# Three split passes for one full-precision product in the second half of a bidirectional recurrence

## The chip, the cores and the metric

The kernel runs on one core of a Trainium2 chip. The metric is the time of one execution on the device in microseconds (us), the median of several runs. Engines are named as in the profile: PE is TensorE's matmul (PEld its load of the stationary operand), DVE is VectorE, ACT is ScalarE, POOL is GpSimd, and SP is SyncE, on whose queue nearly all transfers (DMAs) of this kernel are issued, in program order.

## The reference

One layer over 2048 tokens of width 1024, all in float32: a modulated layer norm, one input projection, two mixers side by side (a bidirectional gated recurrence of 8 heads of 128, and a 2-D neighbourhood attention of 16 heads of 64), one output projection, and a second layer norm. What matters here is one direction of the recurrence for one head:

```python
def step(state, xs):
    qc, kc, vc, dc = xs
    o = jnp.einsum('bhtd,bhdv->bhtv', qc, state)
    state = dc[..., None] * state + jnp.einsum('bhtd,bhtv->bhdv', kc, vc)
    return state, o
...
o = direction(zf_fw, lb_fw, False) + direction(zf_bw, lb_bw, True)
o = _rmsnorm(o.transpose(0, 2, 1, 3), norm_g).reshape(B, S, HG_WIDTH)
return o.astype(g_in.dtype) * jax.nn.silu(g_in)
```

The backward direction runs over the flipped tokens, so the outputs of the first 1024 tokens need a state that comes from the last 1024.

## The kernel before

**Stages.** The program goes through a start (modulation, layer norm, first projections), the attention on the first tokens, the recurrence, the attention on the rest, and the output projection. The recurrence goes over 16 steps: `half` 0 (tokens 0 to 1023) for heads `u` = 0 to 7, then `half` 1 (tokens 1024 to 2047) for the same heads. Each step has two groups `g` of 512 tokens.

**Who sets the order.** `weave` interleaves two generators: `hgrn(u, half, ...)`, the recurrence of one head, and `hgrn_dense`, the projection of the next head (or, in the last step, `border_dense` for the attention that follows). PE's order is what the two generators emit, instruction by instruction, and nothing moves it afterwards (`manual_schedule` for PE). The orders on DVE, ACT, POOL and SP are made by a scheduler when the program is built, which goes by its own estimate of times; so a few more instructions in one place can swap neighbours there.

**Weights.** Each projection matmul in float32 is done in three passes of `fp32r` operands (L278): weights and activations are split into a high part (an ACT copy to `fp32r`) and a low part (a DVE subtraction), and high x high, high x low and low x high are added up in PSUM. Weights come through four raw buffers `wr`, issued on SP at L262, split at L268 (ACT) and L269 (DVE).

**The tail of a head.** After the body of `hgrn`, what is left of a head is handed on as a generator `tail` (`hgrn_tail`), of which the next head's `hgrn` takes a piece at each `next(tail, None)`. Half 0's tail stores, for each group, the output so far (`op_d`, L658), the gate (`sg_d`, L659), and the queries already multiplied by the decay up to the half's end (`qb_d`, L664). Half 1's tail first finishes its own two groups with `rms_out`, and then, with the backward state `R` that its tokens leave behind, goes over the first half's two groups: it loads `qb` (L671), `op` (L672) and the gate (L673), multiplies `R` by `qb` on PE (L676) with both operands as plain float32, adds `op` on DVE (L677) and calls `rms_out`. That one squares on ACT (L345), splits the squares on DVE (L347, L349), sums them over partitions with two `fp32r` matmuls (L354, L355), takes the root on ACT (L357, L358), multiplies on DVE by the output (L359) and by the gate (L361), and stores (L362).

**Buffers.** The three loads are tiles of 128 x 512 under the tag `cl`, for which there are 3 buffers, given out in turn. So group 1's `qb` takes the buffer of group 0's `qb` (free after L676), its `op` takes that of group 0's `op` (free after L359, its last reader), and its gate that of group 0's gate (free after L361). The states `R` are tiles `Sb` with 5 buffers.

Of the kernel before, what the change touches and what calls it, by code (L numbers as in the profile page):

```python
# [10 lines left out]
F32 = mybir.dt.float32  # L11
F32R = mybir.dt.float32r
U32 = mybir.dt.uint32
AF = mybir.ActivationFunctionType
ALU = mybir.AluOpType
# [4 lines left out]
P = 128  # L20
KT = D // P
HALF = 1024
GRP = 512
NHEAD = 8
# [14 lines left out]
def body(ctx: ExitStack, tc: tile.TileContext, t):  # L39
    nc = tc.nc  # L40
    dve, act, pool, pe = nc.vector, nc.scalar, nc.gpsimd, nc.tensor
    dma = nc.sync.dma_start
# [22 lines left out]
    def dram(name, shape, dt=F32):  # L65
        if name in t:
            return t[name]
        return nc.dram_tensor(name, shape, dt, kind="Internal").ap()
# [4 lines left out]
    c_d = dram("c_d", (D,))  # L73
    hs = [dram(f"hs{k}", (P, 2, HALF)) for k in range(KT)]
    op_d = [dram(f"op{i}", (P, HALF)) for i in range(NHEAD)]
    qb_d = [dram(f"qb{i}", (P, HALF)) for i in range(NHEAD)]
    sg_d = [dram(f"sgd{i}", (P, HALF)) for i in range(NHEAD)]
    nq_d = [dram(f"nq{i}", (P, 512)) for i in range(NPAIR)]
    nk_d = [dram(f"nk{i}", (P, 768)) for i in range(NPAIR)]
# [8 lines left out]
    def nm(s):  # L88
        cnt[0] += 1
        return f"{s}_{cnt[0]}"  # L90

    def tl(tag, dt=F32, shape=None):
        if tag in cur["smap"]:
            tag = cur["smap"][tag]
            return sh.tile([P, 512], dt, tag=tag, name=nm(tag), bufs=SH[tag])
        return cur["pool"].tile([P, 512] if shape is None else shape, dt, tag=tag, name=nm(tag), bufs=cur["bufs"].get(tag, 1))
# [4 lines left out]
    def ps(tag="mx"):  # L101
        if tag == "pj":
            return pp.tile([P, 512], F32, tag=tag, name=nm("pj"))
        tag = cur["map"].get(tag, tag)
        return cur["psum"].tile([P, 512], F32, tag=tag, name=nm("ps"), bufs=cur["ps"][tag])
# [237 lines left out]
    def rms_out(u, g, o_sb, sg, tok, rest=False):  # L343
        sq = tl("t")
        act.activation(sq, o_sb, AF.Square)  # L345
        sh_ = tl("rh", F32R)
        dve.tensor_copy(sh_, sq)  # L347
        sl_ = tl("rl", F32R)
        dve.tensor_tensor(sl_, sq, sh_, op=ALU.subtract)  # L349
        yield  # L350
        if rest:
            yield
        pss = ps("ss")
        pe.matmul(pss, ones, sh_, start=True, stop=False)  # L354
        pe.matmul(pss, ones, sl_, start=False, stop=True)  # L355
        r = tl("t")
        act.activation(r, pss, AF.Ln, scale=1.0 / 128.0, bias=eps_rms)  # L357
        act.activation(r, r, AF.Exp, scale=-0.5)  # L358
        dve.tensor_mul(r, r, o_sb)  # L359
        yv = tl("t")  # L360
        dve.tensor_tensor(yv, r, sg, op=ALU.mult)  # L361
        dma(yT[u][:, tok:tok + 512], yv)  # L362
# [60 lines left out]
    def hgrn(u, half, st, tail):  # L423
# [197 lines left out]
        for _ in tail:  # L621
            pass
        return hgrn_tail(u, half, sgs, ubs, decs, qibs, os_, decb_all)

    HSUM = 54

    def hgrn_tail(u, half, sgs, ubs, decs, qibs, os_, decb_all):

        R = None
        if half == 0:  # L630
            ds_ = tl("dsuf", shape=[P, 8])
            pool.memset(ds_[:, 7:8], 1.0)
            for b in range(6, -1, -1):
                dve.tensor_mul(ds_[:, b:b + 1], ds_[:, b + 1:b + 2], decb_all[:, b + 1:b + 2])
        obs = {}
        for g in (1, 0):
            po = os_[g]
            pend = []
            for b in range(3, -1, -1):
                sl = slice(b * P, (b + 1) * P)  # L640
                if R is not None:
                    pend.append((sl, R))
                if half == 0 and g == 0 and b == 0:
                    break
                rn = tl("Sb", shape=[P, P])
                if R is None:
                    dve.tensor_copy(rn, ubs[g][:, sl])
                else:
                    dve.scalar_tensor_tensor(rn, R, decs[1, g][:, b:b + 1], ubs[g][:, sl], op0=ALU.mult, op1=ALU.add)
                R = rn  # L650
            yield
            for sl, r in pend:
                pe.matmul(po[:, sl], r, qibs[1, g][:, sl], start=False, stop=True, skip_group_check=True)
            ob = tl("t")
            act.activation(ob, po, AF.Copy)
            tk = slice(g * 512, (g + 1) * 512)
            if half == 0:
                dma(op_d[u][:, tk], ob)  # L658
                dma(sg_d[u][:, tk], sgs[g])  # L659
                qb = tl("t")  # L660
                for b in range(4):
                    sl = slice(b * P, (b + 1) * P)
                    dve.tensor_scalar(qb[:, sl], qibs[1, g][:, sl], ds_[:, g * 4 + b:g * 4 + b + 1], 1.0, op0=ALU.mult, op1=ALU.mult)
                dma(qb_d[u][:, tk], qb)  # L664
            else:
                yield from rms_out(u, g, ob, sgs[g], HALF + g * 512, g == 0)
        if half == 1:
            for g in range(2):
                tk = slice(g * 512, (g + 1) * 512)
                qb, o1, sg = tl("cl"), tl("cl"), tl("cl")  # L670
                dma(qb, qb_d[u][:, tk])  # L671
                dma(o1, op_d[u][:, tk])  # L672
                dma(sg, sg_d[u][:, tk])  # L673
                yield
                po = ps("pc")
                pe.matmul(po, R, qb, start=True, stop=True)  # L676
                dve.tensor_tensor(o1, po, o1, op=ALU.add)  # L677
                yield from rms_out(u, g, o1, sg, g * 512)

# [777 lines left out]
    with psum_phase("h", *HPS), phase("h", HB, SMH), tc.manual_schedule(engines={mybir.EngineType.PE}):  # L1457
        hgrn_init()
        tail = iter(())
        for i in range(16):  # L1460
            half, u = divmod(i, 8)
# [246 lines left out]
```

## Time and profile before

| | |
|---|---|
| median of 3 runs | 2613.16 us (2608.88 to 2614.05) |
| the profiled execution, its own time | 2611.2 us |
| its span, first to last instruction | 2609.4 us |
| granted TensorE clock, mean | 0.995 |
| PE busy | 2565.7 us (98%) |
| DVE busy | 1741.0 us (67%) |
| ACT busy | 1432.1 us (55%) |
| DMA, mean over the span | 114 GB/s |
| L676, the product with the carried state | 16 products, 32 matmul instructions, 1206.4 to 1717.3 us |

All views are of that one profiled execution, and times in them are counted from its span's start. A busy time of PE is of pipelined matmuls, so PE that is 98% busy may still hold room; the chain of waits shows how long each piece of PE's work really keeps the next one back.

### The profile page before, as it was taken

The page shows a single profiled execution, that of the slowest core. Times are in us where ns is not written, and L with a number is a line of the kernel's source. Part 1 is how long each engine was busy: PE and PEld are TensorE (multiplying, and loading weights), DVE is VectorE, ACT ScalarE, POOL GpSimd, SP SyncE. Part 2 cuts the span into 40 slices and gives each one's busy share as a digit, 9 for nine tenths or more (in the row PEclk, how much of TensorE's full clock was granted, in tenths as well). Part 3 has the DMA queues.
Part 4 walks back from the last instruction along what each step waited for, and adds up shares of the span by engine and source line. Part 5 has one row for each costly group of instructions (what it writes and reads, how often), then busy time and mean ns, then how long its engine had stood idle before and what let it go on. Part 6 is the DMA issues. An engine that isn't in the chain of part 4 may idle for free.

```text
span 2609.4 us, 45888 instructions
## 1 busy us (share of the span) xinstructions
PE 2565.7 (98%) x17180; PEld 2153.9 (83%) x17180; DVE 1741.0 (67%) x4362; ACT 1432.1 (55%) x2853; POOL 108.3 (4%) x143
## 2 busy tenths in 40 slices
PE   8999999999999999999999999999999999999998
PEld 6888788878888888888888888888888887788887
DVE  7445445377777778877778777555777778558443
ACT  5533445376666666666667666455777777431110
POOL 0000000000000000000000000000000000032221
PEclk9999999999999999999999999999999999999999
DMA  7566454212111126212211222354455556444331
GB/s 291 143 207 154 137 177 139 90 50 74 58 65 66 58 78 226 77 49 74 80 62 58 74 73 82 108 147 134 123 143 142 142 138 167 124 152 130 97 97 57
DMA packets 225919, 296.40 MB, mean 114 GB/s; under 512 B 28839, under 2 KB 117543, under 8 KB 224551
## 3 DMA queue, kind: packets, MB, share of 16 engines
q1 hardware_dynamic: 225695, 293.46, 36.8%
q8 instruction: 135, 2.21, 0.4%
q14 instruction: 89, 0.73, 0.1%
HBM read 218.18 MB, written 66.99 MB: 109 GB/s over the span
## 4 chain that ended last, share of the span: by engine, by line
PE 93%; DVE 3%; DMA 2%; ACT 2%; issue 0%; SPq 0%; DVEq 0%; ACTq 0%
PE pj L278 52%; PE pj L291 6%; PE ps L1534 4%; PE ps L1535 4%; PE ps L1533 4%; PE ps L1112 3%; PE ps L1090 3%; PE ps L482 2%; PE ps L474 2%; PE ps L1041 2%; PE ps L549 1%; PE ps L278 1%; PE ps L573 1%; PE ps L1048 1%; PE ps L521 1%; PE ps L575 1%
## 5 line engine op out<-in xcount | busy, mean ns | idle before, releaser
L278 PE MATMUL pj<-h,wh 128*128 128x512 f32 x3984 | 1270.8, 400 | 3.6 <-ACT wh L825 1.9
L278 PEld LDWEIGHTS pj<-h,wh 128*128 128x128 f32 x3984 | 723.4, 189 | 155.4 <-issue 13.8
L278 PE MATMUL pj<-h,wl 128*128 128x512 f32 x1992 | 781.9, 393 | 0.0
L278 PEld LDWEIGHTS pj<-h,wl 128*128 128x128 f32 x1992 | 374.7, 188 | 83.1 <-DVE wl L801 0.4
L1062 ACT ACTIVATE pbuf<-pbuf,mx 128x480 f32<-128x480 f32 (+5 forms) x256 | 152.4, 596 | 109.9 <-DVE mx L1057 109.0
L1057 DVE CUSTOM_DVE_ANT_1 pbuf<-ps,bias 128x480 f32<-128x480 f32 (+5 forms) x256 | 129.1, 540 | 103.1 <-PE ps L1048 46.1
L291 PE MATMUL pj<-wh,h 128*128 128x256 f32 x1024 | 195.7, 286 | 0.3 <-ACT e L774 0.3
L291 PEld LDWEIGHTS pj<-wh,h 128*128 128x128 f32 x1024 | 163.0, 191 | 4.0 <-issue 1.3
L269 DVE TENSOR_TENSOR wl<-wr,wh 128x512 fp32r<-128x512 f32 x192 | 131.6, 686 | 48.0 <-ACT wh L268 47.6
L268 ACT ACTIVATE wh<-wr 128x512 fp32r<-128x512 f32 x192 | 120.0, 626 | 74.2 <-PE pj L278 66.5
L291 PE MATMUL pj<-wl,h 128*128 128x256 f32 x512 | 144.8, 283 | 0.0
L1096 ACT ACTIVATE pt<-ps 120x384 f32<-120x384 f32 (+3 forms) x128 | 65.2, 509 | 121.6 <-PE ps L1090 121.3
L1090 PE MATMUL ps<-ident,pbuf 128*128 128x128 f32 (+2 forms) x832 | 114.4, 275 | 4.5 <-DVE pbuf L1067 3.7
L1094 DVE COPY pt<-ps 120x384 f32<-120x384 f32 (+3 forms) x128 | 74.9, 585 | 63.0 <-PE ps L1090 62.0
L1090 PEld LDWEIGHTS ps<-ident,pbuf 128*128 128x128 f32 (+2 forms) x832 | 97.6, 137 | 22.6 <-issue 2.5
L468 DVE TENSOR_TENSOR de<-e,de 128x512 f32<-128x512 f32 x64 | 44.3, 692 | 95.1 <-ACT de L467 95.1
L1509 ACT ACTIVATE yh<-yr 128x512 fp32r<-128x512 f32 x52 | 32.7, 629 | 133.0 <-PE ps L1534 115.8
L1067 DVE TENSOR_SCALAR pbuf<-pbuf,mx 128x480 f32<-128x480 f32 (+5 forms) x256 | 101.1, 413 | 3.8
L1582 DVE TENSOR_TENSOR vt<-ps,gt 128x512 f32<-128x512 f32 x24 | 16.5, 692 | 130.7 <-PE ps L1535 130.7
L774 ACT ACTIVATE e<-pj 128x512 f32<-128x512 f32 x97 | 57.8, 596 | 79.8 <-PE pj L278 73.1
L291 PEld LDWEIGHTS pj<-wl,h 128*128 128x128 f32 x512 | 97.9, 191 | 1.4 <-issue 0.5
L449 DVE TENSOR_TENSOR_SCAN c<-c,g 128x128 f32<-128x128 f32 x256 | 88.6, 407 | 10.7 <-ACT c L439 10.7
(283 smaller groups left out, 4707.5 us busy)
## 6 DMA issues: line engine op xcount, KB each, us to landing
wr<-in_w_in SPq DMA_DIRECT2D x276, 256.0 KB
yr<-yq SPq DMA_DIRECT2D x64, 256.0 KB
bias<-tint SPq DMA_DIRECT2D x24, 480.0 KB
x<-in_x SPq DMA_DIRECT2D x32, 256.0 KB
ada<-in_ada_m SPq DMA_DIRECT2D x8, 1024.0 KB
wr<-in_w_v SPq DMA_DIRECT2D x32, 256.0 KB
nv<-vt SPq DMA_DIRECT2D x32, 256.0 KB
hs<-s SPq DMA_DIRECT2D x32, 256.0 KB
```

What stands on the lines that cost most here:

```text
L268: act.activation(hi, raw, AF.Copy)
L269: dve.tensor_tensor(lo, raw, hi, op=ALU.subtract)
L278: pe.matmul(pz, a, b, start=(k == 0 and n == 0), stop=(k == KT - 1 and n == 2))
L291: pe.matmul(pzs[tp][:, i * 256:(i + 1) * 256], a, b, start=(k == 0 and n == 0 and i == 0), stop=(k == KT - 1 and n == 2), skip_group_check ...
L449: dve.tensor_tensor_scan(c[:, sl], c[:, sl], L[:, sl], 0.0, op0=ALU.add, op1=ALU.subtract)
L1057: return dve.tensor_tensor_reduce(s[:, 0:nk].rearrange("p (r c) -> p r c", c=kw), sc[:, 0:nk].rearrange("p (r c) -> p r c", c=kw), bt[:, 0 ...
L1062: act.activation(s[:, 0:nk], s[:, 0:nk], AF.Exp, scale=-1.0, bias=mx[:, 0:1], accum_out=mx[:, 1:2])
L1067: dve.tensor_scalar(s[:, 0:nk], s[:, 0:nk], mx[:, 2:3], 1.0, op0=ALU.mult, op1=ALU.mult)
L1090: pe.transpose(ptp[0:cw, c * P:(c + 1) * P], s[:, c * cw:(c + 1) * cw], ident)
L1533: pe.matmul(pz, yh[:, kk], wh, start=first, stop=False)
L1534: pe.matmul(pz, yh[:, kk], wl, start=False, stop=False)
L1535: pe.matmul(pz, yl[:, kk], wh, start=False, stop=last)
```

## The change

In half 0 the decayed queries `qb` are split before they are stored: ACT copies them to `fp32r` (`qh`), DVE subtracts (`ql`), and both are stored, so that `qb_d` has twice the size. In half 1 the state `R` is split on DVE into `Rh` and `Rl`, both queries' parts are loaded, and the one float32 product becomes three `fp32r` products. All of `qh`, `ql`, `op` and the gate are `cl` tiles, four in place of three for 3 buffers; the gate's tile is taken, and its load issued, after the products.

```diff
-    qb_d = [dram(f"qb{i}", (P, HALF)) for i in range(NHEAD)]
+    qb_d = [dram(f"qb{i}", (P, 2, HALF)) for i in range(NHEAD)]
...
-                qb = tl("t")
+                qb, qh, ql = tl("t"), tl("cl", F32R), tl("cl", F32R)
                 for b in range(4):
                     sl = slice(b * P, (b + 1) * P)
                     dve.tensor_scalar(qb[:, sl], qibs[1, g][:, sl], ds_[:, g * 4 + b:g * 4 + b + 1], 1.0, op0=ALU.mult, op1=ALU.mult)
-                dma(qb_d[u][:, tk], qb)
+                act.activation(qh, qb, AF.Copy)
+                dve.tensor_tensor(ql, qb, qh, op=ALU.subtract)
+                dma(qb_d[u][:, 0, tk], qh.bitcast(F32))
+                dma(qb_d[u][:, 1, tk], ql.bitcast(F32))
             else:
                 yield from rms_out(u, g, ob, sgs[g], HALF + g * 512, g == 0)
         if half == 1:
+            Rh, Rl = tl("Sb", F32R, [P, P]), tl("Sb", F32R, [P, P])
+            dve.tensor_copy(Rh, R)
+            dve.tensor_tensor(Rl, R, Rh, op=ALU.subtract)
             for g in range(2):
                 tk = slice(g * 512, (g + 1) * 512)
-                qb, o1, sg = tl("cl"), tl("cl"), tl("cl")
-                dma(qb, qb_d[u][:, tk])
+                qh, ql, o1 = tl("cl", F32R), tl("cl", F32R), tl("cl")
+                dma(qh.bitcast(F32), qb_d[u][:, 0, tk])
+                dma(ql.bitcast(F32), qb_d[u][:, 1, tk])
                 dma(o1, op_d[u][:, tk])
-                dma(sg, sg_d[u][:, tk])
                 yield
                 po = ps("pc")
-                pe.matmul(po, R, qb, start=True, stop=True)
+                for i, (a, b) in enumerate(((Rh, qh), (Rh, ql), (Rl, qh))):
+                    pe.matmul(po, a, b, start=i == 0, stop=i == 2)
+                sg = tl("cl")
+                dma(sg, sg_d[u][:, tk])
                 dve.tensor_tensor(o1, po, o1, op=ALU.add)
                 yield from rms_out(u, g, o1, sg, g * 512)
```

In the changed file the stores stand at L666 and L667, the split of `R` at L672 and L673, the loads of `qh`, `ql`, `op` and the gate at L677, L678, L679 and L685, the products at L683 and the addition at L686; later lines stand 9 lower.

**On SP**, the loads for the two groups of one head in half 1 (head 1). Before, from the store that ends the head's own last group: `cl_2568`, `cl_2569` and `cl_2570` are group 1's `qb`, `op` and gate, and `cl_2717` is the next head's first `qb`.

```order
L362 DMA yq0<-t_2546_13604 128x512 [waits DVE_49]
L671 DMA cl_2568_13736<-qb1 128x512 [waits PE_49]
L262 DMA wr_2679_14251<-in_w_in 128x512 [waits DMAHW3_49,DVE_49]
L262 DMA wr_2682_14257<-in_w_in 128x512 [waits DMAHW4_49,DVE_49]
L672 DMA cl_2569_13737<-op1 128x512 [waits DVE_49]
L362 DMA yq0<-t_2567_13733 128x512 [waits DMAHW5_49,DVE_49]
L673 DMA cl_2570_13738<-sgd1 128x512 [waits DMAHW6_49]
L671 DMA cl_2717_14437<-qb2 128x512 [waits DMAHW7_49,DMAHW1_49,PE_49]
```

Now, the same piece: `cl_2596` is group 0's gate, `cl_2607`, `cl_2608`, `cl_2609` and `cl_2625` are group 1's `qh`, `ql`, `op` and gate.

```order
L362 DMA yq0<-t_2582_13696 128x512 [waits DVE_49]
L685 DMA cl_2596_13782<-sgd1 128x512 [waits PE_49]
L677 DMA cl_2607_13836<-qb1 128x512 [waits PE_49]
L262 DMA wr_2719_14355<-in_w_in 128x512 [waits DMAHW5_49,DVE_49]
L262 DMA wr_2722_14361<-in_w_in 128x512 [waits DMAHW6_49,DVE_49]
L678 DMA cl_2608_13837<-qb1 128x512 [waits DMAHW7_49,DVE_49]
L362 DMA yq0<-t_2606_13833 128x512 [waits DMAHW0_49,DVE_49]
L679 DMA cl_2609_13838<-op1 128x512 [waits DMAHW3_49,DMAHW1_49]
L685 DMA cl_2625_13904<-sgd1 128x512 [waits DMAHW7_49,DMAHW2_49,PE_49]
```

The place in the queue where `op` stood (after the two weight loads, waiting for DVE) now has `ql`; `op` has gone behind the store, to where the gate stood, and group 0's gate is now loaded only after its product.

**On PE**, group 1's product of the same head, before:

```order
L278 MATMUL pj_2584_13778<-h_1886_10379,wl_2583_13775 128x512
L676 MATMUL ps_2585_13800<-cl_2568_13736,Sb_2499_13385 128x512 [waits DMAHW1_49,Activation_49]
L474 MATMUL ps_2589_13809<-ident_71,de_2577_13760 128x128 [waits PE_49]
L474 MATMUL ps_2589_13809<-ident_71,de_2577_13760 128x128 x3
L278 MATMUL pj_2584_13778<-h_1888_10383,wh_2582_13774 128x512
```

and now:

```order
L278 MATMUL pj_2623_13878<-h_1910_10439,wl_2622_13875 128x512
L683 MATMUL ps_2624_13900<-cl_2607_13836,Sb_2583_13699 128x512 [waits DMAHW4_49,Activation_49]
L683 MATMUL ps_2624_13900<-cl_2608_13837,Sb_2583_13699 128x512 [waits DMAHW7_49]
L683 MATMUL ps_2624_13900<-cl_2607_13836,Sb_2584_13700 128x512
L474 MATMUL ps_2629_13913<-ident_71,de_2616_13860 128x128 [waits PE_49]
L474 MATMUL ps_2629_13913<-ident_71,de_2616_13860 128x128 x3
L278 MATMUL pj_2623_13878<-h_1912_10443,wh_2621_13874 128x512
```

The product stands at the same place among the projection matmuls, but its second pass waits for a transfer of its own, that of `ql` (`cl_2608`).

**On ACT**, the square L345 of group 1, in the same head, before:

```order
L476 ACTIVATE ke_2590_13814<-ps_2589_13809 128x512 [waits PE_49]
L467 ACTIVATE de_2661_14171<-c_2641_14094 128x128 x4
L345 ACTIVATE t_2586_13803<-cl_2569_13737 128x512 [waits DVE_49]
L389 ACTIVATE vt_2597_13841<-pj_2584_13778 128x512 [waits PE_49]
L268 ACTIVATE wh_2644_14105<-wr_2643_14103 128x512 [waits DMAHW6_49,PE_49]
```

and now:

```order
L476 ACTIVATE ke_2630_13918<-ps_2629_13913 128x512 [waits PE_49]
L467 ACTIVATE de_2701_14275<-c_2681_14198 128x128 x4
L389 ACTIVATE vt_2637_13945<-pj_2623_13878 128x512 [waits PE_49]
L345 ACTIVATE t_2626_13907<-cl_2609_13838 128x512 [waits DVE_49]
L268 ACTIVATE wh_2684_14209<-wr_2683_14207 128x512 [waits DMAHW0_49,PE_49]
```

L389, the copy of a finished projection out of PSUM, has moved ahead of the square; this stands so in heads 0 to 5, and not in the last two.

## The prediction

> **What bounds the kernel now.** I read the page first, for the span and the chain that ended last.
>
> ```profile
> span 2609.4 us, 45888 instructions
> PE 93%; DVE 3%; DMA 2%; ACT 2%; issue 0%; SPq 0%; DVEq 0%; ACTq 0%
> ```
>
> The chain lies on PE for 93% of the span. The execution took 2611.2 us, 1.8 us more than its span, and is 2.0 us quicker than the median of the runs, 2613.16 us. I sum against the execution and carry the difference over to the median. Next, the engines' busy time by stretches: the first row lies in half 0, the second and third in half 1, the last at the change to the attention.
>
> ```profile
> core 0: us, PE busy (x) PEld busy (x) DVE busy (x) ACT busy (x) POOL busy (x), PEclk, DMA share, GB/s
> 1000.00:1100.00 100.00, 100.00 (x771) 84.73 (x771) 82.49 (x206) 68.43 (x128) 0.10 (x1) 1.00 0.41 138
> 1200.00:1275.00 75.00, 75.00 (x549) 62.36 (x548) 60.02 (x141) 51.17 (x95) 0.00 (x0) 1.00 0.22 71
> 1500.00:1575.00 75.00, 75.00 (x549) 62.34 (x549) 60.03 (x140) 51.16 (x94) 0.00 (x0) 1.00 0.22 71
> 1650.00:1730.00 80.00, 78.59 (x579) 69.11 (x578) 39.28 (x81) 32.64 (x56) 2.07 (x6) 1.00 0.38 113
> ```
>
> In both halves PE is never idle, and DVE and ACT are not full. So what PE is spared comes off the span in full, and every wait that PE gets is added in full; DVE and ACT work counts only where PE must wait for it. The place of the change is read from the chain of waits around head 0's product (start, duration, what):
>
> ```profile
> 1206.60 0.86 PE ps L676 x2
> 1207.46 4.82 PE pj L278 x21
> 1212.28 0.24 PE ps L354
> 1212.51 0.23 PE ps L355
> 1212.75 4.82 PE pj L278 x21
> 1217.57 0.86 PE ps L676 x2
> 1218.43 0.44 PE ps L474 x4
> 1218.86 3.46 PE pj L278 x15
> 1222.32 0.23 PE ps L354
> 1222.56 0.45 PE ps L355
> ```
>
> Group 0's product starts at 1206.60, group 1's at 1217.57, and between them PE has only 10.1 us of other work, with group 0's sums (L354, L355) in the middle.
>
> **The passes.** One product holds PE for 0.86 us. A three-pass `fp32r` product has the form of three projection matmuls; 15 of those took 3.46 us, 0.231 each, so three cost 0.69. That is 0.17 us less, for 16 products 2.7 us less. Both durations are of this kernel, so this term is firm. The Trainium skill, "FP8 and Floating Point Precision", section "TensorE Precision Notes", says that true FP32 goes as four passes through the array; if a pass of those cost a quarter of 0.86 us, leaving one out would give 16 x 0.215 = 3.4 us, and the whole sum would be 0.7 us lower. The rows decide for 2.7.
>
> **The wait for `ql`.** This is the term that decides. `ql` of group 1 takes over the buffer of group 0's `op`, whose last reader is L359, and its load stands on SP where `op` stood. So it is issued when `op` was issued, and lands when `op` landed. But for `op` DVE waited, and for `ql` PE does. The timeline around head 0's group 1:
>
> ```profile
> 1214.47 0.69 DVE L359 TENSOR_TENSOR t<-t,cl 128x512 f32<-128x512 f32 x1 [0.27 <-ACT t L358]
> 1215.19 0.33 SPq L672 DMA_DIRECT2D cl<-op  x1
> 1215.20 0.69 DVE L361 TENSOR_TENSOR t<-t,cl 128x512 f32<-128x512 f32 x1
> 1215.92 0.33 SPq L362 DMA_DIRECT2D yq<-t  x1
> 1216.30 0.42 SPq L673 DMA_DIRECT2D cl<-sgd  x1
> 1218.99 0.69 DVE L677 TENSOR_TENSOR cl<-ps,cl 128x512 f32<-128x512 f32 x1 [3.09 <-DMA cl<-op]
> 1219.39 1.27 ACT L467 ACTIVATE de<-c 128x128 f32<-128x128 f32 x4
> 1220.57 0.62 ACT L345 ACTIVATE t<-cl 128x512 f32<-128x512 f32 x1
> 1221.09 0.58 ACT L389 ACTIVATE vt<-pj 128x512 f32<-128x512 f32 x1
> 1221.76 0.69 DVE L349 TENSOR_TENSOR rl<-t,rh 128x512 fp32r<-128x512 f32 x1
> ```
>
> L359 ends at 1215.16, the load goes out at 1215.19, and DVE starts L677 at 1218.99, after 3.09 us of idling that ended with this load. PE took up the product at 1217.57, 2.41 us after L359's end. With 0.23 for the first pass, it asks for `ql` 2.64 us after L359's end. How late the load was over all heads is in the view of waits (who waited for whom: total, times, longest), for the recurrence's second half:
>
> ```profile
> DVE cl L677 <- DMA cl<-op: 17.4, 6, 3.9
> DVE cl L677 <- PE ps L676: 4.9, 2, 2.6
> PEld ps L355 <- DVE rl L349: 3.0, 8, 0.4
> ```
>
> In six heads the load came last, in two PE did. The last head is one of the six, and its rows are these (the third is PE's):
>
> ```profile
> 1715.61 0.69 DVE L359 TENSOR_TENSOR t<-t,cl 128x512 f32<-128x512 f32 x1 [0.70 <-ACT t L358]
> 1719.94 0.69 DVE L677 TENSOR_TENSOR cl<-ps,cl 128x512 f32<-128x512 f32 x1 [1.49 <-DMA cl<-op]
> 1716.90 1.02 PE L676 MATMUL ps<-cl,Sb 128*128 128x512 f32 x2
> ```
>
> The other five idled (17.4 - 1.49) / 5 = 3.18 us from L361's end, which is 0.73 after L359's: the load was usable 3.91 us after L359's end, and PE would have waited 3.91 - 2.64 = 1.27 us in each, 6.4 in all. In the two others it was there by 2.45 + 0.73 = 3.18: a wait between 0 and 0.54, taken as 0.3 each, 0.6. In the last head PE comes only 0.6 after L359's end, and would wait from 1716.90 + 0.23 to 1719.94, 2.8 us. The sum is 9.8 us. If all eight were like the two quick ones it would be 8 x 0.54 = 4.3; if the two quick ones were like the five, 11.7. Behind the waiting pass on PE stands everything, transposes and projections, so nothing makes this up.
>
> **The square behind L389.** In heads 0 to 5 ACT now copies a projection (L389) before group 1's square L345. The chain from L345 over L349 to PE's L355 has no room: in all eight heads PE waits for L349, 0.4 us at most, and L355 took 0.45 in place of 0.23. L345 starts as soon as L467 leaves ACT; pushed behind L389 it starts 0.52 us later (1220.57 to 1221.09), and PE waits that much more, 6 x 0.52 = 3.1 us. At the least it is 0 (if L345 comes later for another reason, whose wait is counted already), at the most 6 x 0.58 = 3.5. `op` lands later too, by its new place behind the store; the gate's load stood there at 1216.30, 1.1 us after `op`'s, so L677 would start near 1220.1 where PE's own shift allows about 1219.5. It still ends before ACT is through with L389, and costs nothing more.
>
> **The change to the attention.** The last head's tail feeds what comes after it. ACT's splits of the first keys come behind L358 in its order, and these keys' last copy was what PE waited for (a piece of the chain, then the idle time before the first scores, L1041):
>
> ```profile
> 1733.25 9.30 DMA KB<-KB
> ...
>   DMA KA<-KA: 1.5, 1
>   DMA KB<-KB: 0.8, 1
> ```
>
> PE already waits 2.3 us there, so a later tail is passed on. PE's own 2.8 us shift in the last head covers most of it; `op`'s later landing and the copy's new place on SP behind two stores of values are not covered. I bound this by 0 and 3 us and take 1.
>
> **Half 0.** Per group ACT gets one more copy and DVE one more subtraction, SP one more store; the nearest rows for the two are those of the weights' split, in the groups of half 0.
>
> ```profile
> L269 DVE TENSOR_TENSOR wl<-wr,wh 128x512 fp32r<-128x512 f32 x102 | 69.9, 687 | 19.8 <-ACT wh L268 19.5
> L268 ACT ACTIVATE wh<-wr 128x512 fp32r<-128x512 f32 x102 | 63.7, 625 | 33.1 <-PE pj L278 32.8
> ...
> L476 ACT ACTIVATE ke<-ps 128x512 f32<-128x512 f32 x32 | 19.0, 594 | 45.1 <-PE ps L474 45.1
> ```
>
> That is 16 x 0.63 = 10 us of ACT and 16 x 0.69 = 11 us of DVE, spread over a stage where DVE was busy for 82.49 of 100 us in the stretch shown first. The chain that leads to PE begins at L476, and the last row shows ACT idle before it for 45.1 us in all, always for PE: 1.4 us each time, over twice one added copy. No gain is possible, as PE waits for neither engine there; I take 0, and 3 us if the cover fails at some heads. The stores' waits on SP hold up weight loads behind them, which have four raw buffers of lead. In half 1 the split of `R` is two DVE instructions of 128 x 128 per head, made in an earlier piece of the tail than the product, and costs nothing; group 0's `qh`, `ql` and `op` are loaded a head earlier, and its gate, now loaded after the product, is wanted only at L361, 7.7 us after.
>
> **The sum.** -2.7 + 9.8 + 3.1 + 1.0 + 0 = +11.2 us: 2622.4 us for the profiled execution, 2624.4 us for the median. With the low ends, -2.7 + 4.3 = +1.6, 2614.8 us; with the high ends, -2.7 + 11.7 + 3.5 + 3 + 3 = +18.5, 2631.7 us.
>
> **Rivals.** *The load comes in time.* PE asks 2.64 us after L359's end; if `ql` is there by then, the wait is gone in seven heads.
>
> ```profile
> 1702.37 2.01 DMA yq<-t
> ```
>
> For it: this store of the same 256 KB was through in 2.01 us, and 2.9 us would do for nearly all. The point that decides is thus 2.6 us from issue to landing. Against it: the two weight loads issued just ahead of `op` stay where they are, and six of eight were later. With the wait gone but for the last head's, partly (1 of 2.8 us), and ACT's swap still there at half (1.5): -2.7 + 1 + 1.5 = -0.2, 2613.0 us: not slower. The Trainium skill, "DMA: Bandwidth & Descriptors", section "Anatomy of one DMA", gives about 2.0 us plus the bytes at 436 GB/s, which for 256 KB is 2.6 us, just at that point. The trace does not agree for these loads: 3.8 us from issue to use in head 0.
>
> *Only the passes count.* If the scheduler's order left every cover whole, the result were -2.7, 2610.5 us, still within 0.2%. The order on PE and SP speaks against it.
>
> *Half 0's cover fails too.* With ACT and DVE late at each of 16 groups by 0.3 us, 5 more: +16, 2629 us. For it is DVE at 82%; against it, the 1.4 us before L476.
>
> *Faster by over 0.2%.* It would need twice the passes' gain, and no row holds it.
>
> **Chances.** The forecast has 0.79, of which 0.06 lie under +5.2 us; the load in time 0.10, only the passes 0.04, half 0's failure 0.05, a gain 0.02. About 0.2%, 5.2 us, is what a measurement of this kernel can tell from no change. So slower 0.73 + 0.05 = 0.78, same 0.06 + 0.10 + 0.04 = 0.20, faster 0.02. The range takes nearly all of the forecast's own, 2614.8 to 2631.7, and half 0's failure: 2614.5 to 2631.
>
> **What would show it.** Right: PE waits at L683 for `cl<-qb` about 1.2 us in most heads, and 2.8 in the last; the wait of L355 for L349 rises from 0.4 to 0.9 in six heads; L677 no longer idles 3 us for `op` alone; half 0 ends when it did. Wrong: PE does not wait at L683, or only group 0's product does; half 0 is longer; or the span grows in the attention stage, which the change does not touch.

## The result

Six runs of the changed kernel gave a median of 2628.95 us (2623.03 to 2631.89), six of the kernel before 2613.45 us. The ratio is 1.0068, with an interval of 1.0058 to 1.0078: slower, by 15.5 us between the medians and by 17.8 us by the ratio, where 11.2 were foretold. The median lies in the stated range; by the ratio the time is 2631.2 us, 0.2 over its upper end. The profiled execution took 2631.89 us, the longest of the six, so its trace shows more than the usual loss: 20.7 us of span over the trace before.

The page of the changed kernel, the span and the chain that ended last:

```profile
span 2630.1 us, 46055 instructions
PE 86%; DVE 6%; DMA 4%; ACT 3%; issue 1%; SPq 0%; DVEq 0%; ACTq 0%
```

PE's share of the chain fell from 93% to 86%, and DMA, DVE and ACT took what it lost. Where it fell is in the stretches (busy time of each engine), the same four as before:

```profile
1000.00:1100.00 100.00, 100.00 (x771) 84.72 (x770) 83.60 (x207) 69.75 (x131) 0.10 (x1) 1.00 0.43 144
1200.00:1275.00 75.00, 73.16 (x522) 60.94 (x522) 58.80 (x137) 49.23 (x92) 0.00 (x0) 1.00 0.25 76
1500.00:1575.00 75.00, 73.32 (x498) 61.04 (x487) 58.81 (x138) 49.67 (x93) 0.00 (x0) 1.00 0.25 78
1650.00:1730.00 80.00, 77.91 (x654) 68.74 (x653) 41.57 (x91) 32.90 (x58) 2.08 (x6) 1.00 0.36 110
```

In half 0 PE is as full as before; in half 1, where 75 us are about one head, it now lacks 1.8 and 1.7 of them. The chain of waits around head 0's group 1 shows why:

```profile
1214.86 0.70 DVE t L359
1215.58 4.17 DMA cl<-qb
1219.75 0.04 issue
1219.80 0.73 PE ps L683 x2
1220.53 0.45 PE ps L474 x4
...
1222.76 0.48 ACT vt L389
1223.25 0.53 ACT t L345
...
1223.80 0.44 DVE rh L347
...
1224.26 0.70 DVE rl L349
1224.96 0.04 issue
1225.01 0.51 PE ps L355
```

Before, this piece was PE from end to end. Now the chain leaves PE for the end of L359, the load of `ql` that L359's buffer held back, and only then comes to the second pass; below it L389 stands ahead of the square, as the order said. PE's view of waits in the recurrence's second half (first the matmuls', then the weight loads'):

```profile
PE ps L683 <- DMA cl<-qb: 15.9, 8, 3.0
PE ps L355 <- DVE rl L349: 1.3, 6, 0.2
```

```profile
PEld ps L683 <- DMA cl<-qb: 19.1, 8, 3.3
...
PEld ps L355 <- DVE rl L349: 3.6, 7, 0.5
PEld ps L354 <- DVE rh L347: 1.5, 5, 0.3
```

Every one of the eight second passes waits. The 15.9 us count from the first pass's modelled end, 0.39 us after its start; the next pass could have begun at 0.23, so the path lost 15.9 + 8 x 0.16 = 17.2 us. Of the 20.7 us this and the passes' own -2.7 make 14.5.

### The profile page after: what moved, and what is told of

It reads as the page before. It is cut to its first block, busy times and chain, and to the rows that moved or that the text cites. A ratio compares the mean times of both kernels' runs of the same rounds, so it can differ in the third digit from the quotient of the medians.

```text
span 2630.1 us, 46055 instructions
## 1 busy us (share of the span) xinstructions
PE 2566.6 (98%) x17196; PEld 2157.1 (82%) x17196; DVE 1753.9 (67%) x4394; ACT 1440.2 (55%) x2869; POOL 108.9 (4%) x143
## 4 chain that ended last, share of the span: by engine, by line
PE 86%; DVE 6%; DMA 4%; ACT 3%; issue 1%; SPq 0%; DVEq 0%; ACTq 0%
PE pj L278 46%; PE pj L291 6%; PE ps L1543 4%; PE ps L1542 4%; PE ps L1544 4%; PE ps L1121 3%; PE ps L1099 3%; PE ps L482 2%; PE ps L1050 2%; PE ps L474 1%; PE ps L549 1%; PE ps L278 1%; DMA cl<-qb 1%; PE ps L1057 1%; PE ps L521 1%; DMA bias<-tint 1%
## 5 line engine op out<-in xcount | busy, mean ns | idle before, releaser
L1542 PE MATMUL ps<-wh,yh 128*128 128x512 f32 x240 | 93.4, 389 | 0.0
```

Source lines behind the costliest of these rows:

```text
L1542: pe.matmul(pz, yh[:, kk], wh, start=first, stop=False)
```

## The experiments

My theory: the loss is PE's wait for `ql` of group 1, whose load can't go out before L359 releases a buffer. Rivals: the added work (half 0, the order on ACT, the attention's start), the distance of the rows in DRAM, and the split operands or the passes as such. Intervals are of the ratio to the kernel before.

**Four buffers.**

```
-    "cl": 3
+    "cl": 4
```

> The changed kernel with four buffers for `cl` in place of three, nothing else. `ql` of group 1 then takes a buffer that PE itself freed one product earlier, and its load no longer stands behind L359. Late load (my theory: 18 of the 20.7 us are PE waiting at the second pass for `ql` of group 1, and the rest of the half-1 loss follows from that): the wait at L683 goes to 0 in all eight heads, PE's two-instruction product becomes 0.69 us, and the time comes to the time before less 2 to 3 us: ratio to before 0.998 to 0.9995. Rival, the added work (split and stores in half 0, the square behind L389, the copy behind two stores at the change to the attention): these stay, and with the wait gone the ratio is still 1.001 to 1.003.

Ratio 0.9998 (0.9990 to 1.0007). The chain of waits at the same place:

```profile
1213.89 2.96 PE pj L278 x13
1216.85 0.69 PE ps L683 x3
1217.54 0.44 PE ps L474 x4
1217.97 3.44 PE pj L278 x15
1221.42 0.23 PE ps L354
1221.65 0.47 PE ps L355
```

PE never leaves it, the three passes take 0.69 us as worked out, and L355 comes as early after L354 as before. The loss is gone, while the three passes, half 0's splits and stores and the slower start of the attention are still there: the theory stands, and these three fall as causes. The order on ACT is not among them: in this run's trace the square L345 stands ahead of L389 again in heads 0 to 5, so four buffers undo the late load and the swap on ACT together. The 2 to 3 us of gain did not quite come; the waits of PE in half 1 say where they stayed:

```profile
PE ps L1050 <- DMA KA<-KA: 3.3, 1, 3.3
PE pj L291 <- ACT vt L299: 2.2, 2, 2.1
```

The first is the start of the attention, 4.2 us with the second copy's 0.9 against 2.3 before. The second is new: in the last head ACT stood idle at the square for `op`, which was still late, and PE needed a copy behind it.

**Without the load of `ql`.**

```
-                dma(ql.bitcast(F32), qb_d[u][:, 1, tk])
-    ((Rh, qh), (Rh, ql), (Rl, qh))
+    ((Rh, qh), (Rh, qh), (Rl, qh))
```

> The changed kernel without the load of `ql`: the second pass reads `qh` again (part of the computation left out), three passes stay, half 0 still splits and stores both halves; three `cl` tiles per group as before the change. Late load: no wait at L683, ratio 0.998 to 0.9995, as with four buffers; this is what the passes alone are worth, -2.7 us, plus what half 0 costs. If half 0's additions cost something, the ratio stays above 1.0005.

Ratio 0.9995 (0.9986 to 1.0003), with no wait at the products. Three passes without a late operand cost nothing that this run can tell, and neither does half 0 with its splits and stores. The gain of 2.7 us does not show in full; as with four buffers, L345 stands ahead of L389 again, PE waits 2.2 us for a copy in the last head, and 5.0 us at the start of the attention. That an on-time load of `ql` costs anything can't be told from this: the two intervals overlap almost wholly.

**Rows 4 KB apart.**

```
-    qb_d: one tensor (P, 2, HALF) per head
+    qh_d, ql_d: two tensors (P, HALF) per head
```

> The changed kernel with `qh` and `ql` stored in two tensors in DRAM with rows 4 KB apart, as `op` has them, in place of one with rows 8 KB apart; three buffers as in the change. Rival, row distance: `ql` landed 4.3 us after its issue where `op` from the same place in the queue took 3.6, because its rows lie 8 KB apart; with 4 KB it lands 0.5 to 0.7 us sooner, the waits of group 1 fall from 18 us to 12 to 14 us, ratio 1.004 to 1.005. Queue theory (the later landing comes from the loads and stores around it): landing and waits stay within 0.15 us each, ratio 1.0055 to 1.0075.

Ratio 1.0049 (1.0036 to 1.0063), 2621.09 us against 2610.26. PE's waits, and the load in the chain of head 0:

```profile
PE ps L684 <- DMA cl<-ql: 9.5, 8, 2.1
```

```profile
1215.47 3.88 DMA cl<-ql
```

The wait fell from 15.9 to 9.5 us, 0.8 a head, with the queue and the buffer as in the change. Not all of the 6.4 us need come from the rows: the next run has the loads of the change, and its wait, with the later pass added back, is 11.9 + 1.8 = 13.7 us, 4.2 above this one. So 4 to 6 us of the wait went with the second tensor. That it was the distance of the rows, and not the tensors' place in DRAM, which changed with it, is not shown. It is not the whole loss: this kernel is still slower by 10.8 us. In the time, the interval overlaps that of the change (1.0058 to 1.0078).

**`ql` in the last pass.**

```
-    ((Rh, qh), (Rh, ql), (Rl, qh))
+    ((Rh, qh), (Rl, qh), (Rh, ql))
```

> The changed kernel with the pass that reads `ql` last of the three (Rh qh, Rl qh, Rh ql). Late load: PE asks for `ql` one pass, 0.23 us, later, so each wait shrinks by 0.23 us: 8 x 0.23 = 1.8 us less than the changed kernel, ratio to before 1.0045 to 1.006. If it is not the landing of the load that holds the second pass but the pass itself (a pass that follows another into the same sums), nothing changes or the third pass shows the same 2 us.

Ratio 1.0060 (1.0046 to 1.0074), PE's wait down to 11.9 us. PE's timeline at head 0:

```profile
1216.95 0.63 PE L683 MATMUL ps<-cl,Sb 128*128 128x512 f32 x2
1219.06 0.50 PE L683 MATMUL ps<-cl,Sb 128*128 128x512 f32 x1 [1.48 <-DMA cl<-qb]
```

Now two passes go through back to back, and the third waits: it is the operand and not the pass that is waited for. The wait fell by 4.0 us where 1.8 follow from the pass's place (the loads also landed sooner: in the mean of the eight heads `ql` was usable 4.12 us after L359's end, in the change 4.34); in the time, 1.0068 to 1.0060, nothing certain shows.

**`qb` in the late buffer, first attempt.** In the kernel before:

```
-    qb, o1, sg = tl("cl"), tl("cl"), tl("cl")
+    tiles = tl("cl"), tl("cl"), tl("cl")
+    qb, o1, sg = tiles if g == 0 else (tiles[1], tiles[0], tiles[2])
```

> The kernel before the change (one FP32 product, one `qb`, rows 4 KB apart), with one thing altered: for group 1 `qb` and `op` swap their `cl` buffers, so that `qb` takes the buffer which L359 releases and `op` the early one. Late load: the FP32 product of group 1 then waits as the changed kernel's second pass did. PE asks 2.24 us after L359's end and a load from there landed 3.6 us after its issue, so 1.3 to 1.4 us in seven heads and near 3 us in the last: 12 to 13 us, less up to 3 us where `op` now comes early: ratio 1.0035 to 1.005. Rival, the split operands or the three passes are what PE waits on: with neither here, the ratio is 0.999 to 1.001.

Ratio 1.0003 (0.9993 to 1.0012): a miss of the edit, not of a theory. The waits of DVE still have `op` late, in six heads as before (not all the same ones):

```profile
DVE cl L678 <- DMA cl<-op: 16.1, 6, 3.4
```

So `op` still had the late buffer. The next edit changes the order of the loads instead of the names.

**`qb` in the late buffer, by the order of the loads.** Again in the kernel before:

```
-    dma(qb, ...); dma(o1, ...)
+    for g == 1: dma(o1, ...); dma(qb, ...)
```

> The kernel before the change with the two loads of group 1 written in the other order (`op`, then `qb`); the earlier attempt to swap their buffers left the order as it was, since a buffer is given to the tile that is written first. Now `qb` takes the buffer released by L359, in the place where `op` stood on SP, and `op` the early one; one FP32 product, rows 4 KB apart, no split. Late load: PE asks 2.24 us after L359's end and `op` landed there 3.6 us after its issue, so 1.4 us in seven heads and 3.0 in the last, 12 to 13 us of waiting at L676: ratio 1.0035 to 1.005. Rival, it takes the split operands or several passes to make PE wait: ratio 0.999 to 1.001.

Ratio 1.0048 (1.0034 to 1.0062), 2621.24 us against 2608.65. PE's waits, and the piece of the chain in head 0:

```profile
PE ps L677 <- DMA cl<-qb: 11.2, 8, 2.5
```

```profile
1214.22 0.70 DVE t L359
1214.92 0.02 issue
1214.94 3.52 DMA cl<-qb
1218.46 0.14 issue
1218.59 1.10 PE ps L677 x2
```

One FP32 product, no split, nothing new in half 0, and the same wait at the same place. L345 stands ahead of L389 here, as before. With the edge counted as in the change, 8 x 0.16 us, the wait is 12.5 us, and the ratio makes 12.5 us of time. The theory alone foretold this: whichever operand of the product takes L359's buffer, PE waits for it. With it the rival of the split operands and the passes is gone, and neither 8 KB rows nor the swap on ACT is needed for a loss.

**`op` in rows 8 KB apart.** In the kernel before, a single run:

```
-    op_d = dram((P, HALF))
+    op_d = dram((P, 2, HALF)), first half used
```

> The kernel before the change with `op` stored in rows 8 KB apart instead of 4 KB, nothing else. Row distance: `op` of group 1, 3.6 us from issue to landing before, takes 4.1 to 4.4 us, and DVE idles at L677 about 0.7 us longer each time. If the 0.7 us came from something else in the changed kernel (the place of the tensor, the other transfers), it stays at 3.6.

2609.74 us in one run, among 2604.38 to 2617.11 of the kernel before. The waits of DVE at the addition:

```profile
DVE cl L677 <- DMA cl<-op: 22.1, 7, 3.9
DVE cl L677 <- PE ps L474: 2.6, 1, 2.6
```

The load came last in seven heads in place of six, and DVE's idling for it rose from 17.4 to 22.1 us: 0.6 us a head, or 0.3 with the heads in which PE came last (22.3 to 24.7 us in all). The direction is that of the two tensors, the size smaller than the 0.7 expected, and not certain: the first attempt above, with `op` in rows 4 KB apart, had 16.1 us and 21.1 in all, so two executions with the same loads differ by 1.2. The one time taken shows no loss, as expected where `op`'s lateness falls on DVE and is covered; `ql`'s falls on PE.

**Four buffers in the kernel before.**

```
-    "cl": 3
+    "cl": 4
```

> The kernel before the change with four `cl` buffers in place of three, nothing else: `op` of group 1 is then loaded early, as with five in the changed kernel. If the late `op` had cost time before (L355's waits, 3 us, and part of the last head's 3 us): ratio 0.9975 to 0.9995. If its lateness was covered: 0.9995 to 1.0005. The passes' own worth is the difference to the five-buffer run, by the sum 2.7 us or 0.001.

Ratio 0.9996 (0.9987 to 1.0004). No load is waited for at L677 any more (what is left is PE's), and the time is the same: `op`'s lateness was covered before. So a fourth buffer is worth nothing to the old kernel that these runs can tell.

**Five buffers in the changed kernel.**

```
-    "cl": 3
+    "cl": 5
```

> The changed kernel with five `cl` buffers. With four, `ql` was early but group 1's `op` still waited for L359; in the last head the square L345 stood 3.8 us idle for it and PE then waited 2.2 us for a copy behind it. With five, `op` takes a buffer that PE frees too. Late load carried further: no wait at L683 nor 3 us at L686, the wait of L355 for L349 goes, and the last head's 2.2 us go: ratio 0.997 to 0.999. Rival, the change to the attention (the keys' copy behind the bias rows) takes back what the recurrence gives: ratio 0.9993 to 1.0005, with a longer wait at the first scores.

Ratio 0.9982 (0.9973 to 0.9991), 2603.95 us against 2607.77: faster than both kernels. PE's waits in half 1 and at the start of the attention, all of them:

```profile
PE ps L1050 <- DMA KA<-KA: 2.4, 1, 2.4
PE pj L291 <- ACT e L783: 0.3, 1, 0.3
```

The last head's 2.2 us are gone with `op`'s lateness, and the attention's start is back at 2.4. One part of the expectation failed: L355 still waits for L349 as before, 2.8 us in the weight loads' view, so that wait doesn't come from `op`.

**Five buffers, two tensors, `ql` last.**

> All three together: five `cl` buffers, `qh` and `ql` in two tensors with rows 4 KB apart, the pass with `ql` last. Late load: with five buffers the loads are a whole projection ahead, so nearer rows and a later pass add nothing: the same as five buffers alone, ratio 0.9973 to 0.9991. If transfers themselves still cost PE something, it is lower by 0.0005 or more.

Ratio 0.9980 (0.9971 to 0.9989): the same as five buffers alone. Once the loads are early, neither the rows nor the order of the passes makes a difference that these runs can tell; what they did in the change, they did through the wait.

## Why the prediction was right or wrong

**What bounds.** Right: PE was full, and its waits came into the time in full, most plainly with `qb` in the late buffer: 12.5 us of waits, 12.5 us of time.

**The passes.** Right, 0.69 us for three where nothing waits. Behind a wait the two that are left take 0.73, where two without one take 0.63 (the timeline with `ql` last), 0.1 a head that the sum did not have. The five-buffer kernel against the four-buffer kernel before, 0.9982 to 0.9996, is 3.7 us by the ratios, with intervals that hold 2.7.

**The wait for `ql`.** The mechanism was right, the place and the direction too; the size was not: 9.8 us foretold, 17.2 measured. The step that failed reads "So it is issued when `op` was issued, and lands when `op` landed". The first half held: the load went out 0.03 us after L359's end, as before. The second did not: in the mean of the eight heads `ql` was usable 4.34 us after L359's end (3.80 to 4.91), where the terms of the sum come to 3.69. That is 0.65 x 8 = 5.2 us. `op`'s rows lie 4 KB apart, those of the new `qb` tensor 8 KB, which was in the diff, and I took the transfer by its bytes and its place alone. With two tensors and rows at 4 KB the mean is 3.61 and the wait 9.5 + 8 x 0.16 = 10.8 us, near the 9.8; with `ql` last, at 8 KB, the mean is 4.12, so some 0.2 of the 0.65 may be scatter between executions. The second slip is PE's question: I took it from the chain's row for the product, 2.41 us after L359's end, and the first pass really starts at 2.24 in heads 0 to 5, and at 1.79 in head 6: 1.6 us more of waiting. The rest, 0.5, lies in heads 2 and 6, for which the sum took 0.3 us each of a possible 0.54.

The bound of 11.7 for this term was too low, as it took only `op`'s own scatter for the load's; the wait passed it by 5.5 us. That the median still lies in the range is luck as far as this term goes: the high end also held 3 us for half 0, which cost nothing. And the range was closed at 2631, a little under the 2631.7 of its own high ends.

**The square behind L389.** Right in kind: in head 0 L355 starts 0.73 us after L354 where 0.34 passed before (timeline of PE in each kernel).

```profile
1224.28 0.49 PE L354 MATMUL ps<-rh,ones 128*128 128x512 f32 x1
1225.01 0.51 PE L355 MATMUL ps<-rl,ones 128*128 128x512 f32 x1 [0.23 <-DVE rl L349]
```

That is 0.39 us. It stands so in heads 0 and 2 to 5, 1.9 us in five, for the 3.1 foretold in six. In head 1, where PE ran at a lower clock just then (last section), L355 starts 0.23 after L354, sooner than before. `op` did land later, as foretold: DVE idled 33.3 us for it at L686, in head 0 until 1221.12, well ahead of the square at 1223.15, so that this cost nothing there. With four buffers the square stands ahead of L389 again, and L355 comes as early as before.

**The change to the attention.** PE waited there for the copies of keys as follows:

```profile
PE ps L1050 <- DMA KA<-KA: 3.6, 1, 3.6
PE ps L1050 <- DMA KB<-KB: 0.8, 1, 0.8
```

4.4 us against 2.3: 2.1 for the 1.0 taken, within 0 to 3. In the last head the wait of L354 for L347, 1.0 us before, is gone: PE came later by itself, which the sum did not have.

**Half 0.** Right, as far as the trace can tell: half 1's first product starts 0.5 us later, at 1206.9 in place of 1206.4, and the other runs here have it between 1204.7 and 1206.8. The split's rows in half 0 are those expected, and ACT's slack before L476 fell from 45.1 to 42.0 us only:

```profile
L476 ACT ACTIVATE ke<-ps 128x512 f32<-128x512 f32 x32 | 19.1, 595 | 42.0 <-PE ps L474 42.0
L664 ACT ACTIVATE cl<-t 128x512 fp32r<-128x512 f32 x16 | 10.1, 633 | 5.2 <-DVE t L663 5.2
```

**The sum.** -2.7 + 17.2 + 1.9 + 2.1 - 1.0 = +17.5 us of the profiled 20.7. Two pieces of the other 3.2 us can be placed: the passes behind the wait, 8 x 0.1 = 0.8, and the stretch in head 1 at half the clock, 3.41 us long, which does 1.7 us less work. Whether the change as such is to be charged with the second is open, as over the whole span both kernels have the same mean clock, 0.995. The 0.7 us left stay open too; the runs of one kernel differ by more. Of the rivals, the load in time was the wrong way round (loads landed later than in the trace before, not sooner), half 0's failure did not come, and "only the passes" is what four and five buffers made of it. The 2.6 us that the prediction works out for the first of these from the Trainium skill, "DMA: Bandwidth & Descriptors", section "Anatomy of one DMA", comes from a fit of loads issued on the GpSimd path, while these go out on SP; in the change they were usable 3.8 to 4.9 us after their issue.

## What to carry to other kernels

When a load moves from one consumer to another, ask which engine now waits: the same late buffer cost DVE's addition nothing that these runs could tell, and PE's product 11 to 17 us. Count the tiles that one step of a loop takes from a tag and the buffers that are free when the next step loads; a fourth tile in three buffers chained the load of PE's operand to the last reader of the group before, and two more buffers turned a loss of 0.7% into a gain of 0.2%. A transfer's duration may be borrowed from another only with room for what differs: here tensor, rows and execution together moved a load of about 4 us by 0.2 to 0.7 us a head, and eight heads made that the largest error of the forecast.

## What the runs showed of the hardware

The 256 KB load of `ql`, in rows of 2 KB, was usable 4.34 us after L359's end in the change and 4.12 with `ql` last, both with rows 8 KB apart in DRAM, and 3.61 with two tensors and rows 4 KB apart (means of eight heads): 0.5 to 0.7 us sooner. For `op` alone the difference was 0.3 to 0.6, not clear of the scatter. The Trainium skill, "DMA: Bandwidth & Descriptors", section "Latency and other measured facts", lists slower copies only for row pitches of 512 KB and more; no run here goes there, and these show a difference at far smaller ones, whose cause they don't show.

In head 1 the wait before the second pass was followed by a stretch at a lower granted clock. The trace's records of the clock change only at whole multiples of 3.413 us from one another; there are 136 of them from this fall at 1298.07 to the next at 1762.28. So the rows below are cut into such steps (busy time by stretches, the clock in the column after POOL's):

```profile
1294.65:1298.06 3.41, 1.13 (x8) 0.81 (x7) 0.00 (x0) 0.00 (x0) 0.00 (x0) 1.00 0.58 208
1298.07:1301.48 3.41, 3.41 (x10) 2.74 (x9) 1.67 (x3) 2.76 (x7) 0.00 (x0) 0.50 0.49 154
1448.25:1451.66 3.41, 1.61 (x8) 0.99 (x6) 0.00 (x0) 0.00 (x0) 0.00 (x0) 1.00 0.73 225
1731.56:1734.97 3.41, 1.91 (x16) 1.59 (x14) 2.08 (x3) 0.90 (x2) 0.00 (x0) 1.00 0.62 135
1734.97:1738.38 3.41, 1.91 (x14) 1.82 (x15) 0.57 (x1) 0.00 (x0) 0.00 (x0) 1.00 0.81 264
```

In the first row PE is idle for 2.3 of 3.4 us, and over the next step the clock is 0.50. The third row is head 3's wait: idle for 1.8 us, and the clock stays at 1.00 behind it. The last head's wait is longer, 3.0 us, but a step's end cuts it into 1.5 and 1.5 (the last two rows), and no fall follows. The twelve traces of this case agree, counted in these steps from 40 us on: 64 of 67 falls followed a step in which PE was idle for 1.8 us or more (the other three 1.5), and of the steps idle for over 1.9 us one alone, at 1.92, had no fall behind it. These are idle times by modelled ends of matmuls. The Trainium skill, "TensorE: Matmul & The Clock Gate", section "Part 1: The HAM clock gate", has the clock fall after an idle window of about 3.4 us, with windows that run freely. The traces agree with the free run and the length, and not with a whole idle window: here about half of one was enough.
